# Seven-product v, u and y over super-blocks of 1024 tokens, and LN's small steps for four row tiles at once

## The chip, the cores and the metric

One Trainium2 chip; the kernel runs on one of its cores. The metric is the device time of one execution in microseconds. The core has a matrix engine (TensorE, PE in the profile, with its weight loads as PEld), VectorE (DVE), ScalarE (ACT), GpSimd (POOL) and SyncE (SP), which issues the DMAs here. Each engine works through its own instructions strictly in the order in which they stand and waits at semaphores for the others. TensorE writes to PSUM, eight banks of 128 x 512 float32; the tiles lie in SBUF, 128 partitions wide.

## What is computed

One decoder layer on 2048 tokens of width 1024, all in float32. The mixer is a gated MLP:

```python
h = x * (1.0 + sc1) + sh1                       # sc1, sh1, g1, ... = silu(c) @ mod_w + mod_b
z = gelu(h @ w_in + b_in); u, v = split(z)      # h @ w_in: 2048x1024 by 1024x2048
v = layer_norm(v)                               # over 1024 columns
sv = causal(w_s) @ v, per chunk of 128 tokens and group of 128 columns, + b_s
y = (u * sv) @ w_out                            # 2048x1024 by 1024x1024
x = layer_norm(ALPHA * x + (1.0 + g1) * y)      # "LN1"
h = x * (1.0 + sc2) + sh2
x = layer_norm(ALPHA * x + (1.0 + g2) * ((silu(g) * u2) @ ffn_w_out))   # g, u2 = split(h @ ffn_w_in)
```

## The kernel before

Every float32 operand of a product is split in two parts (`parts`, L90 to L95): ScalarE casts the tile to the matmul's rounded type and VectorE takes the rest, `src - cast`. A product is then three matmuls (hi x hi, hi x lo, lo x hi: `HL`). One matmul is 128 x 128 weights by 128 x 512 columns.

The mixer runs over four blocks of 512 tokens (`NB`, `TB`). In each block `v_part` makes v with `token_major` (8 steps of 24 matmuls into all eight banks, L190 to L206), `us_part` makes u with `feature_major` (8 tiles of 24 matmuls, L208) and, between them, the spatial product `s_tile` and `yT = parts(sv * u)`; `y_part` makes y with `token_major` again. That is 192 matmuls each for v, u and y in a block. The weights wv, wu and wo are loaded and split anew in each block (`load_w`, L97).

LN1 of a block (`norm` in `y_part`, L352 to L367) is done row tile by row tile, 128 tokens each, while TensorE is in the next block's v product: VectorE scales by g1, adds x and takes statistics; `norm_of` (L154) makes the factor with eight small steps on 128 x 1 values, the power on GpSimd; ScalarE normalises; GpSimd multiplies by ln1g and adds ln1b (L364, L366). `h2_part` (L371) transposes the normalised rows on TensorE for the FFN, in the middle of the next block's u (step `h` in the list of L330); the last block's rows are read back from memory in the FFN (`tail`). While the first three blocks run, 48 columns of the modulation are made on VectorE from 512 KB loads each (`mod_col`, L119).

The FFN is already in the seven-product form (Strassen's scheme in Winograd's variant): `h2_part` and `weight` make the sums of quarters on GpSimd (`sub`, L84). It starts with `f_0g_X`, after y's last matmul.

A scheduler orders each engine's instructions when the program is built, from the order of the calls, the tiles' free buffers and its own estimate of times; on the chip the order is fixed. Tiles come from pools with a fixed number of buffers per tag: a new tile waits until the oldest of its tag is released. `late` has 12 buffers of 128 x 1024.

Of the kernel before, what the change touches and what calls it, by code (L numbers as in the profile page):

```python
# [8 lines left out]
F32 = mybir.dt.float32  # L9
# [4 lines left out]
P = 128  # L14
D = 1024
# [21 lines left out]
def gmlp_swiglu_layer(  # L37
# [21 lines left out]
    for side, pad in (("left", 448), ("right", 480)):  # L59
        pads = ctx.enter_context(tc.tile_pool(name=f"pad_{side}", bufs=1, side=side))  # L60
        nc.vector.memset(pads.tile([P, pad // 4], F32, name=f"pad_{side}"), 0.0)
# [34 lines left out]

    def load_w(src, name, tag="raw"):  # L97
        r = new(tag, f"{name}_raw")
        nc.sync.dma_start(out=r, in_=src)
        return [parts(r[:, h * 512 : (h + 1) * 512], f"{name}_{h}", "w") for h in range(2)]  # L100
# [73 lines left out]

    def stats_tile(name, groups=2):
        return small.tile([P, groups, 6], F32, tag=f"st{groups}", name=f"{name}_st", bufs=20 if groups == 2 else 1)
# [13 lines left out]
    def token_major(operands, nk, name, between=()):  # L190

        ps = [[bank(f"{name}_ps{t}{h}") for h in range(2)] for t in range(NT)]
        for k, (a, w) in enumerate(operands):
            for t in range(NT):
                for part, wpart in HL:
                    for h in range(2):
                        nc.tensor.matmul(  # L197
                            ps[t][h],
                            lhsT=a[:, part, t * P : (t + 1) * P],
                            rhs=w[h][:, wpart, :],  # L200
                            start=(k == 0 and part == 0 and wpart == 0),
                            stop=(k == nk - 1 and part == 1),
                        )
            for f in between[k :: nk]:
                f()
        return ps  # L206

    def feature_major(w, rhs, name):  # L208

        ps = bank(name)  # L210
        n = 0
        for d in range(ND):
            for wpart, part in HL:
                nc.tensor.matmul(  # L214
                    ps,
                    lhsT=w[d // 4][:, wpart, (d % 4) * P : (d % 4 + 1) * P],
                    rhs=rhs[d][:, part, :],
                    start=(n == 0),
                    stop=(n == 3 * ND - 1),
                )  # L220
                n += 1
        return ps
# [6 lines left out]
    def start():  # L229
        cact = new("cact", "cact")  # L230
# [7 lines left out]
    def setup_spatial():  # L238

        wm = new("bcv", "wm")  # L240
# [7 lines left out]
        lb = new("raw", "lnb_bc")  # L248
        nc.sync.dma_start(out=lb, in_=lnb.partition_broadcast(P))
        bsr = new("raw", "bs_row")  # L250
        nc.sync.dma_start(out=bsr[0:1, :], in_=bs)
        tb = new("bcv", "tb")
# [10 lines left out]
    def v_operands(b, hT):  # L263
        def operands(d):
            if b == 0:
                sh1[d] = mod_col(0, d, 0.0, "first")
                sc1[d] = mod_col(1, d, 1.0, "first")
            r = new("xh" if b else "first", f"xT{b}_{d}", HALF)
            nc.sync.dma_start(out=r, in_=xT[d, :, b * TB : (b + 1) * TB])
            nc.vector.tensor_scalar(r, r, sc1[d], sh1[d], ALU.mult, ALU.add)  # L270
            hT.append(parts(r, f"hT{b}_{d}", "hT"))
            return hT[d], load_w(wv[d * P : (d + 1) * P, :], f"wv{b}_{d}", "raw" if b else "first")

        return ahead([lambda d=d: operands(d) for d in range(ND)])

    def v_part(b, operands, between):
        ps = token_major(operands, ND, f"v{b}", between)
        if b == 0:
            env["first"].close()
            env["mix"] = phase("left", yT=(8, UNIT), raw=(3, ROW), bcv=(3, ROW), vrow=(4, ROW))  # L280
            env["bv"] = bcast(bv, "bv_bc", "bcv")
# [493 lines left out]
```

## Time and profile before

| what | value |
|---|---|
| median of three runs | 1934.01 us (1925.23 to 1934.22) |
| the profiled execution | 1927.45 us |
| its span, from first to last instruction | 1925.7 us |
| TensorE busy | 1850.6 us, 96% of the span |
| VectorE busy | 1271.0 us, 66% |
| ScalarE, GpSimd busy | 760.3 us, 725.6 us |
| DMA | 312.8 MB, 162 GB/s on average |
| mean granted TensorE clock | 0.983 of full speed |

The mixer takes the first 602 us, the FFN's first product (into `aop`) runs to some 1440 us, the second one and the last LN to the end. Busy times are means over stages with different limits; an engine's idle time matters only where the engine that sets the end waits for it.

### The profile page before, as it was taken

Reading aid. Unit: us, or ns where it says so; the run is one execution under the profiler, and the core shown is the slowest. Engines: PE = TensorE matmul, PEld = TensorE weight load, DVE = VectorE, ACT = ScalarE, POOL = GpSimd, SP = SyncE. Lnnn points to the kernel's source line nnn. Section 1 sums busy time; section 2 is a strip of 40 time slices with the busy share of each in tenths; the row PEclk is TensorE's granted clock in tenths of the full one; section 3 lists DMA queues with packets and bytes.
Section 4 is the critical chain, followed back from the end, with each engine's and each line's share of the span. In section 5 each row is a group of like instructions: output and inputs, shape, how many; then the busy total and the mean of one; then the engine's idle time right before and its main releaser. Section 6 shows DMA issues by size and latency. Waiting matters only on the chain.

```text
span 1925.7 us, 23473 instructions
## 1 busy us (share of the span) xinstructions
PE 1850.6 (96%) x8297; PEld 1532.6 (80%) x8297; DVE 1271.0 (66%) x1857; ACT 760.3 (39%) x1251; POOL 725.6 (38%) x465
## 2 busy tenths in 40 slices
PE   7999999999999999999999999999999999999766
PEld 6887788878888788888887888888888888887655
DVE  8587867686758956555668565556554433576998
ACT  3542543633545434333345333333343444332331
POOL 0000500550402666645644554456432200244844
PEclk9999999999999999999999999999999999999978
DMA  9359446464455444542336323323347644555542
GB/s 354 127 188 326 163 153 227 154 229 158 147 181 186 144 157 153 175 147 94 104 123 202 113 104 115 104 88 110 110 150 253 210 137 142 169 174 171 187 158 109
DMA packets 135065, 312.77 MB, mean 162 GB/s; under 512 B 16642, under 2 KB 21026, under 8 KB 134947
## 3 DMA queue, kind: packets, MB, share of 16 engines
q1 hardware_dynamic: 134882, 311.24, 47.8%
q8 instruction: 65, 1.06, 0.2%
q14 instruction: 54, 0.43, 0.1%
q0 software_dynamic: 64, 0.03, 0.0%
HBM read 239.37 MB, written 71.84 MB: 162 GB/s over the span
## 4 chain that ended last, share of the span: by engine, by line
PE 78%; DVE 13%; DMA 5%; issue 2%; POOL 1%; ACT 1%; SPq 0%; DVEq 0%; POOLq 0%; ACTq 0%
PE o L582 17%; PE u_ps L214 7%; PE y_ps L197 6%; PE v_ps L197 5%; DVE modw L123 2%; PE f_5u_X L433 1%; PE f_4u_X L433 1%; PE f_3u_X L433 1%; PE f_2u_X L433 1%; PE f_9u_X L433 1%; PE f_9g_X L433 1%; PE f_8u_X L433 1%; PE f_8g_X L433 1%; PE f_7u_X L433 1%; PE f_7g_X L433 1%
## 5 line engine op out<-in xcount | busy, mean ns | idle before, releaser
L582 PE MATMUL o<-wd_w,alw 128*128 128x512 f32 (+1 forms) x1881 | 427.9, 390 | 34.9 <-DVE o L82 29.5
L582 PEld LDWEIGHTS o<-wd_w,alw 128*128 128x128 f32 x1881 | 353.8, 191 | 108.9 <-ACT alw L93 23.9
L197 PE MATMUL v_ps<-wv,hT 128*128 128x512 f32 x768 | 179.5, 396 | 16.0 <-ACT wv L93 11.9
L94 DVE TENSOR_TENSOR alw<-al,alw 128x512 fp32r<-128x512 f32 x154 | 126.6, 855 | 94.1 <-ACT alw L93 92.3
L197 PEld LDWEIGHTS v_ps<-wv,hT 128*128 128x128 f32 x768 | 146.5, 191 | 48.1 <-ACT wv L93 12.1
L214 PE MATMUL u_ps<-hT,wu 128*128 128x512 f32 x768 | 181.9, 396 | 0.7 <-ACT h L388 0.5
L197 PE MATMUL y_ps<-wo,yT 128*128 128x512 f32 x768 | 177.0, 392 | 3.9 <-DVE sv L320 3.9
L197 PEld LDWEIGHTS y_ps<-wo,yT 128*128 128x128 f32 x768 | 144.9, 189 | 34.3 <-issue 4.3
L214 PEld LDWEIGHTS u_ps<-hT,wu 128*128 128x128 f32 x768 | 144.9, 191 | 31.3 <-issue 0.8
L161 POOL TENSOR_TENSOR ln_rs<-ln_ve,mhalf 128x1 f32<-128x1 f32 x32 | 27.3, 860 | 357.5 <-DVE ln_ve L159 346.2
L93 ACT CAST alw<-al 128x512 fp32r<-128x512 f32 x154 | 88.8, 619 | 146.3 <-PE o L582 117.7
L85 POOL TENSOR_TENSOR chain<-wd,chain 128x512 f32<-128x512 f32 x22 | 34.6, 1576 | 157.4 <-DMA wd<-in_wd 154.6
L94 DVE TENSOR_TENSOR wu<-wu_raw,wu 128x512 fp32r<-128x512 f32 x64 | 59.5, 946 | 50.5 <-ACT wu L93 50.1
L93 ACT CAST wv<-wv_raw 128x512 fp32r<-128x512 f32 x64 | 37.6, 620 | 98.0 <-PE v_ps L197 43.0
L123 DVE SCALAR_TENSOR_TENSOR modw<-modw,cact 128x1024 f32<-128x1024 f32 x48 | 58.3, 1218 | 19.0 <-DMA modw<-in_modwT 19.0
L94 DVE TENSOR_TENSOR wv<-wv_raw,wv 128x512 fp32r<-128x512 f32 x64 | 47.5, 761 | 21.8 <-ACT wv L93 21.7
L94 DVE TENSOR_TENSOR wo<-wo_raw,wo 128x512 fp32r<-128x512 f32 x64 | 46.8, 742 | 19.8 <-ACT wo L93 19.8
L94 DVE TENSOR_TENSOR wd_w<-wd,wd_w 128x512 fp32r<-128x512 f32 x44 | 37.1, 842 | 34.5 <-ACT wd_w L93 34.5
L93 ACT CAST wo<-wo_raw 128x512 fp32r<-128x512 f32 x64 | 38.5, 616 | 43.2 <-PE y_ps L197 42.1
L93 ACT CAST wu<-wu_raw 128x512 fp32r<-128x512 f32 x64 | 38.1, 616 | 35.2 <-PE v_ps L197 18.9
L93 ACT CAST wd_w<-wd 128x512 fp32r<-128x512 f32 x44 | 27.3, 621 | 47.7 <-PE o L582 35.7
L364 POOL TENSOR_TENSOR r<-r,ln1g_bc 128x1024 f32<-128x1024 f32 x16 | 42.4, 2665 | 10.0 <-ACT r L173 10.0
(606 smaller groups left out, 3870.7 us busy)
## 6 DMA issues: line engine op xcount, KB each, us to landing
al<-aop SPq DMA_DIRECT2D x154, 256.0 KB, 3.3
wd<-in_wd SPq DMA_DIRECT2D x99, 256.0 KB, 3.3
modw<-in_modwT SPq DMA_DIRECT2D x48, 512.0 KB, 8.1
aop<-aop_s SPq DMA_DIRECT2D x88, 256.0 KB, 2.0
wv_raw<-in_wv SPq DMA_DIRECT2D x32, 512.0 KB, 5.0
wu_raw<-in_wu SPq DMA_DIRECT2D x32, 512.0 KB, 4.1
wo_raw<-in_wo SPq DMA_DIRECT2D x32, 512.0 KB, 3.6
hop<-h SPq DMA_DIRECT2D x40, 256.0 KB, 3.1
```

Source lines behind the costliest of these rows:

```text
L85: nc.gpsimd.tensor_tensor(out=o, in0=a, in1=b, op=ALU.subtract)
L93: nc.scalar.copy(out=o[:, 0, :], in_=src)
L94: nc.vector.tensor_tensor(out=o[:, 1, :], in0=src, in1=o[:, 0, :].bitcast(F32), op=ALU.subtract)
L123: nc.vector.scalar_tensor_tensor(out=w, in0=w, scalar=1.0, in1=env["cact"], op0=ALU.mult, op1=ALU.mult, accum_out=modc[:, j : j + 1],)
L161: nc.gpsimd.tensor_tensor(out=rs, in0=ve, in1=mhalf, op=ALU.pow)
L197: nc.tensor.matmul(ps[t][h], lhsT=a[:, part, t * P : (t + 1) * P], rhs=w[h][:, wpart, :], start=(k == 0 and part == 0 and wpart == 0), sto ...
L214: nc.tensor.matmul(ps, lhsT=w[d // 4][:, wpart, (d % 4) * P : (d % 4 + 1) * P], rhs=rhs[d][:, part, :], start=(n == 0), stop=(n == 3 * ND ...
L364: nc.gpsimd.tensor_tensor(out=r, in0=r, in1=env["ln1g"], op=ALU.mult)
L433: nc.tensor.matmul(ps, lhsT=w[:, wpart, k * P : (k + 1) * P], rhs=a[k][:, part, :], start=(first and k == 0 and wpart == 0 and part == 0), ...
L582: nc.tensor.matmul(ps[:, cs], lhsT=a[:, part, p * P : (p + 1) * P], rhs=w[:, wpart, cs], start=(first and part == 0 and wpart == 0), stop= ...
```

## The change

The mixer runs over two super-blocks of 1024 tokens (`mixer(sb, before)`), and v, u and y are each made by seven products on quarters: 512 tokens x 512 inputs (four tiles of 128 inputs, `k`) by 512 inputs x 512 outputs, 48 matmuls each, 12 per `k`. `left_ops` makes the sums of the left quarters (of h, shared by v and u, and of u * sv), `right_ops` those of the weights, both on GpSimd; `combine` adds up the results, on VectorE from PSUM and, after products 6 and 7, on GpSimd from SBUF. The order is `SEVEN`, v and u in turn up to product 3, then v 7, v 4, u 7, u 4. The spatial tiles of a super-block's first half stand in u 7, those of the second in u 4 and y 1. LN1 of the first half is called after y's product 3 and its `h2_part` in y's product 4; LN1 of the second half in the next super-block's v 1 and u 1, its `h2_part` in v 2. `norm_rows` makes the factors of four row tiles in one set of small steps on 128 x 4 values, for the LN of v and LN1; it begins when all four have their statistics. The modulation's columns are all made in the first super-block. The FFN is as before.

```diff
+    def norm_rows(tiles, sts, name):
+        m = len(tiles)
+        mv = sm("mvs", [m, 2])
+        for t in range(m):
+            nc.vector.bn_aggr(out=mv[:, t, :], in_=sts[t])
+        ve, rs, nw, nm = (sm(tag, [m]) for tag in ("ves", "rss", "nws", "nms"))
+        nc.vector.tensor_scalar(ve, mv[:, :, 1], EPS, None, ALU.add)
+        nc.gpsimd.tensor_tensor(out=rs, in0=ve, in1=mhalf.broadcast_to([P, m]), op=ALU.pow)
...
+        for t in range(m):
+            nc.scalar.activation(tiles[t], tiles[t], AF.Identity, bias=nm[:, t : t + 1], scale=rs[:, t : t + 1])
...
+    SEVEN = (1, 2, 5, 6, 3, 7, 4)
+    def left_ops(raw, name):
...
+            if pr == 5:
+                a21, a22 = quarter(1, 0, k), quarter(1, 1, k)
+                s1[k] = new("half", f"{name}_s1{k}")
+                nc.gpsimd.tensor_tensor(out=s1[k], in0=a21, in1=a22, op=ALU.add)
+                sub(a21, a11, a21)
+                sub(a11, s1[k], a11)
+                sub(a12, a12, a11)
+            src = {1: (0, 0), 6: (0, 0), 2: (0, 1), 3: (0, 1), 7: (1, 0), 4: (1, 1)}.get(pr)
+            return parts(a[(*src, k)] if src else s1[k], f"{name}_S{pr}{k}", "S")
+    def right_ops(w, name):
...
+            if pr == 5:
+                t = chain[k] = load(0, 1, k, "chain")
+                sub(t, t, load(0, 0, k))
+            elif pr in (6, 4):
+                t = chain[k]
+                sub(t, load(1, 1 if pr == 6 else 0, k), t)
+            elif pr == 7:
+                t = load(1, 1, k)
+                sub(t, t, load(0, 1, k))
+            else:
+                t = load(1 if pr > 1 else 0, 1 if pr == 3 else 0, k)
+            return parts(t, f"{name}_T{pr}{k}", "w")
+    def combine(pr, ps, cell, bias=None):
+        for j in range(4):
...
+            else:
+                add(cell(1, 0, j), ps[j], cell(1, 0, j))
+            if pr in (6, 7):
+                o = cell(*((0, 1) if pr == 6 else (1, 1)), j)
+                nc.gpsimd.tensor_tensor(out=o, in0=cell(1, 0, j), in1=cell(1, 1, j), op=ALU.add)
...
+        steps = [(m, pr) for pr in SEVEN[:5] for m in "vu"] + [("v", 7), ("v", 4), ("u", 7), ("u", 4)]
...
+        during["u", 7] = s_tiles(0, *range(8))
+        during["u", 4] = s_tiles(1, *range(4, 8))
+        made = ahead([lambda m=m, pr=pr, k=k: operands(m, pr, k) for m, pr in steps for k in range(NK)], 3)
...
+        for pr in SEVEN:
+            ps = [bank(f"y{sb}_{pr}_{j}") for j in range(4)]
+            if pr == 4:
+                during[4] = h2_parts(blocks[0], [rows[0, t] for t in range(NT)])
...
+            combine(pr, ps, cell_y)
+            if pr == 3:
+                for f in norms(blocks[0], [rows[0, t] for t in range(NT)]):
+                    f()
...
+        def final():
+            norm_rows(rows, sts, f"ln1_{b}")
+            for t, r in enumerate(rows):
+                nc.gpsimd.tensor_tensor(out=r, in0=r, in1=env["ln1g"], op=ALU.mult)
+                e = nc.vector if b == NB - 1 else nc.gpsimd
+                e.tensor_tensor(out=r, in0=r, in1=env["ln1b"], op=ALU.add)
...
+    mix = phase(
+        "left", S=(10, UNIT), w=(5, UNIT), braw=(4, HALF), chain=(8, HALF), bc=(4, ROW), h2=(2, ROW), sv=(2, HALF),
+    )
+    early = phase("right", half=(26, HALF))
...
+    rows = mixer(0, before)
+    steps = norms(1, rows)
+    before = {("v", 1): steps[:NT], ("u", 1): steps[NT:], ("v", 2): h2_parts(1, rows)}
+    rows = mixer(1, before)
```

How the instructions stand now is told at three places. In the names, `v0_5_2` is v of super-block 0, product 5, fourth-part 2; `h0_S51` a split left operand of product 5, k 1; `wv0_T51` a split right one; `r0_3` row tile 3 of block 0 for LN1.

GpSimd at the start of the first super-block. Before, the first row is the causal mask of w_s (`wm`), and after it come the powers of LN:

```order
L243 AFFINE_SELECT wm_746<-wm_746 128x1024
L161 TENSOR_TENSOR lnv0_0_rs_824<-lnv0_0_ve_822,mhalf_83 128x1
L161 TENSOR_TENSOR lnv0_1_rs_883<-lnv0_1_ve_881,mhalf_83 128x1
L161 TENSOR_TENSOR lnv0_2_rs_942<-lnv0_2_ve_940,mhalf_83 128x1
L161 TENSOR_TENSOR lnv0_3_rs_962<-lnv0_3_ve_960,mhalf_83 128x1
```

Now, in the same place (`xT0_0` and its like are the scaled h quarters, `wv0_b010` weight quarters):

```order
L313 AFFINE_SELECT wm_509<-wm_509 128x1024
L226 TENSOR_TENSOR h0_s10_767<-xT1_0_761,xT1_4_764 128x512
L85 TENSOR_TENSOR xT1_0_761<-xT0_0_342,xT1_0_761 128x512
L85 TENSOR_TENSOR wv0_b010_775<-wv0_b010_775,wv0_b000_777 128x512
L85 TENSOR_TENSOR xT0_0_342<-h0_s10_767,xT0_0_342 128x512
L85 TENSOR_TENSOR wv0_b011_817<-wv0_b011_817,wv0_b001_819 128x512
L85 TENSOR_TENSOR xT0_4_545<-xT0_4_545,xT0_0_342 128x512
L226 TENSOR_TENSOR h0_s11_809<-xT1_1_803,xT1_5_806 128x512
```

Between the mask and the first power of LN there now stand 50 sums of 128 x 512.

TensorE at the transposes of block 0's rows. Before, they stand among block 1's u tiles:

```order
L214 MATMUL u1_3_ps_2183<-hT1_7_1887,wu1_3_1_2113 128x512 x3
L387 MATMUL h2T0_0_ps_2211<-ident_76,r0_0_1562 128x128
L387 MATMUL h2T0_0_ps_2211<-ident_76,r0_1_1563 128x128
L387 MATMUL h2T0_0_ps_2211<-ident_76,r0_2_1564 128x128
L387 MATMUL h2T0_0_ps_2211<-ident_76,r0_3_1565 128x128
```

Now they stand behind y's last product of the super-block, in the order of the rows and over all eight banks, and the next super-block's v comes after them:

```order
L267 MATMUL y0_4_2_2782<-wo0_T43_2790,y0_S43_2784 128x512 x3
L267 MATMUL y0_4_3_2783<-wo0_T43_2790,y0_S43_2784 128x512 x3
L497 MATMUL h2T0_0_ps_2806<-ident_76,r0_0_2325 128x128
L497 MATMUL h2T0_4_ps_2812<-ident_76,r0_0_2325 128x128
L497 MATMUL h2T0_1_ps_2833<-ident_76,r0_0_2325 128x128
```

The end of the same run of 32 transposes, whose last eight read r0_3:

```order
L497 MATMUL h2T0_6_ps_2866<-ident_76,r0_3_2331 128x128
L497 MATMUL h2T0_3_ps_2887<-ident_76,r0_3_2331 128x128
L497 MATMUL h2T0_7_ps_2893<-ident_76,r0_3_2331 128x128
L267 MATMUL v1_1_0_2942<-wv1_T10_2917,h1_S10_2912 128x512 x3
L267 MATMUL v1_1_0_2942<-wv1_T11_2928,h1_S11_2923 128x512 x3
```

The transposes of block 2 stand in the same way between y's last product of the second super-block and the FFN's first matmul, where before the FFN followed y at once.

GpSimd at LN1 of block 0. Before, each row tile has its own power and its multiplication and addition follow:

```order
L161 TENSOR_TENSOR ln1_0_3_rs_1826<-ln1_0_3_ve_1824,mhalf_83 128x1
L364 TENSOR_TENSOR r0_0_1562<-r0_0_1562,ln1g_bc_1234 128x1024
L364 TENSOR_TENSOR r0_1_1563<-r0_1_1563,ln1g_bc_1234 128x1024
L364 TENSOR_TENSOR r0_2_1564<-r0_2_1564,ln1g_bc_1234 128x1024
L366 TENSOR_TENSOR r0_0_1562<-r0_0_1562,ln1b_bc_1236 128x1024
```

Now:

```order
L182 TENSOR_TENSOR ln1_0_rss_2656<-ln1_0_ves_2655,mhalf_83 128x4
L468 TENSOR_TENSOR r0_0_2325<-r0_0_2325,ln1g_bc_1513 128x1024
L468 TENSOR_TENSOR r0_1_2327<-r0_1_2327,ln1g_bc_1513 128x1024
L468 TENSOR_TENSOR r0_2_2329<-r0_2_2329,ln1g_bc_1513 128x1024
L470 TENSOR_TENSOR r0_0_2325<-r0_0_2325,ln1b_bc_1515 128x1024
L468 TENSOR_TENSOR r0_3_2331<-r0_3_2331,ln1g_bc_1513 128x1024
L470 TENSOR_TENSOR r0_1_2327<-r0_1_2327,ln1b_bc_1515 128x1024
L470 TENSOR_TENSOR r0_2_2329<-r0_2_2329,ln1b_bc_1515 128x1024
L182 TENSOR_TENSOR ln1_1_rss_3079<-ln1_1_ves_3078,mhalf_83 128x4
L470 TENSOR_TENSOR r0_3_2331<-r0_3_2331,ln1b_bc_1515 128x1024
```

Block 1's power (`ln1_1_rss`) has moved ahead of block 0's last addition. In block 2 both powers stand first, and r2_3's addition is the twelfth wide operation behind them.

## Rows read from the trace of the kernel before

**Rows 1.** Stage table: length, busy time and count of each engine, clock, DMA share, GB/s.

```profile
core 0: us, PE busy (x) PEld busy (x) DVE busy (x) ACT busy (x) POOL busy (x), PEclk, DMA share, GB/s
0.00:602.00 602.00, 578.41 (x2689) 481.55 (x2690) 434.64 (x804) 260.73 (x407) 126.34 (x86) 0.99 0.57 198
700.00:1400.00 700.00, 697.50 (x3089) 577.16 (x3088) 416.02 (x463) 275.30 (x472) 364.85 (x232) 1.00 0.37 125
```

**Rows 2.** Timeline of TensorE: start, length, engine, line, output and inputs, count.

```profile
11.88 46.08 PE L197 MATMUL v_ps<-wv,hT 128*128 128x512 f32 x192 [11.88 <-ACT wv L93]
...
63.97 29.11 PE L214 MATMUL u_ps<-hT,wu 128*128 128x512 f32 x120
...
504.12 22.02 PE L214 MATMUL u_ps<-hT,wu 128*128 128x512 f32 x96
525.98 3.65 PE L387 MATMUL h2T_ps<-ident,r 128*128 128x128 f32 x32
...
558.35 43.78 PE L197 MATMUL y_ps<-wo,yT 128*128 128x512 f32 x192
601.97 2.88 PE L433 MATMUL f_0g_X<-h2A,f_0g_w 128*128 128x512 f32 x12
```

**Rows 3.** Timeline of VectorE in the first block, GpSimd idle.

```profile
6.64 1.23 DVE L123 SCALAR_TENSOR_TENSOR modw<-modw,cact 128x1024 f32<-128x1024 f32 x1 [5.32 <-DMA modw<-in_modwT]
...
14.30 1.22 DVE L123 SCALAR_TENSOR_TENSOR modw<-modw,cact 128x1024 f32<-128x1024 f32 x1
...
15.44 0.33 DVE L127 TENSOR_SCALAR modc<-modc,modbc 128x1 f32<-128x1 f32 x2
15.81 0.55 DVE L270 TENSOR_SCALAR xT<-xT,modc 128x512 f32<-128x512 f32 x1
16.27 1.29 DVE L94 TENSOR_TENSOR wv<-wv_raw,wv 128x512 fp32r<-128x512 f32 x2
17.48 1.22 DVE L123 SCALAR_TENSOR_TENSOR modw<-modw,cact 128x1024 f32<-128x1024 f32 x1
```

**Rows 4.** Timelines of GpSimd and of VectorE in the same 3 us of the FFN.

```profile
764.17 1.28 POOL L411 TENSOR_TENSOR aop_s<-aop_s,f_3g_c 128x512 f32<-128x512 f32 x1
765.42 1.74 POOL L85 TENSOR_TENSOR f_4g_b<-f_4g_b,f_4g_b 128x512 f32<-128x512 f32 x1
...
764.30 1.71 DVE L94 TENSOR_TENSOR f_4u_w<-f_4u_b,f_4u_w 128x512 fp32r<-128x512 f32 x1
765.93 1.77 DVE L503 TENSOR_TENSOR f_3g_u<-f_3g_u,f_3u_u 128x512 f32<-128x512 f32 x1
```

**Rows 5.** Groups by line: count, busy us, mean ns of one, idle before.

```profile
L364 POOL TENSOR_TENSOR r<-r,ln1g_bc 128x1024 f32<-128x1024 f32 x12 | 31.4, 2632 | 8.5 <-ACT r L173 8.5
L173 ACT ACTIVATE r<-r,ln_nm,ln_rs 128x1024 f32<-128x1024 f32 x12 | 14.2, 1235 | 3.9 <-DVE ln_nm L172 3.8
L286 DVE TENSOR_TENSOR v<-v_ps,bv_bc 128x512 f32<-128x512 f32 x32 | 20.0, 676 | 7.8 <-PE v_ps L197 7.8
L166 DVE TENSOR_TENSOR lnv_rs<-lnv_rs,lnv_nw 128x1 f32<-128x1 f32 x16 | 2.3, 153 | 0.0
```

**Rows 6.** The same stretch, line L94 on VectorE alone: its busy time and count.

```profile
700.00:1400.00 700.00, 286.38 (x283) 1.00 0.37 125
```

**Rows 7.** The tail, 1800 to 1926 us: stage table, then VectorE's groups by line.

```profile
1800.00:1926.00 126.00, 84.99 (x382) 70.24 (x380) 117.51 (x171) 31.78 (x46) 69.86 (x41) 0.83 0.40 139
...
L94 DVE TENSOR_TENSOR alw<-al,alw 128x512 fp32r<-128x512 f32 x26 | 27.2, 1064 | 1.0 <-ACT alw L93 1.0
L539 DVE TENSOR_TENSOR o<-o,ln2b_bc 128x1024 f32<-128x1024 f32 x12 | 21.7, 1809 | 2.4 <-POOL o L538 2.4
...
L166 DVE TENSOR_TENSOR ln_rs<-ln_rs,ln_nw 128x1 f32<-128x1 f32 x12 | 9.8, 822 | 0.6 <-DVE ln_nw L165 0.5
...
L164 DVE SCALAR_TENSOR_TENSOR ln_nw<-ln_rs,ln_ve 128x1 f32<-128x1 f32 x11 | 8.7, 788 | 0.2 <-POOL ln_rs L161 0.2
```

**Rows 8.** DMA issues: queue, count, KB each, median us from issue to landing.

```profile
x<-in_x SPq DMA_DIRECT2D x16, 512.0 KB, 6.5
```

**Rows 9.** Stage table around the tail's gap on TensorE, columns as in rows 1.

```profile
1840.00:1850.00 10.00, 5.44 (x11) 3.38 (x12) 10.00 (x12) 2.79 (x5) 7.54 (x6) 0.52 0.66 233
```

## What the change does to the time: the prediction

> **What bounds the kernel now.** I read the stage table first. Up to 602 us, where the mixer ends, TensorE is busy for 578 us, and in the FFN's first product (700 to 1400) for 697.5 of 700 us: TensorE's instruction stream sets the time. VectorE works 435 us and GpSimd only 126 us in the mixer; ScalarE has 261 us [rows 1]. TensorE's own timeline gives the pieces, each row a run of like matmuls. 192 matmuls of 512 columns take 43.62 us from start to start (558.35 to 601.97), so 0.2272 us each. A block's spatial products and h2 transposes are the rest of 504.12 to 558.35: 54.23 - 43.62 = 10.6 us, of which the transposes take 3.6 and s_tile's matmuls 7.0; the first block also has 6.1 us of small matmuls for tb before its u products [rows 2]. The FFN's first matmul stands at 601.97 us. Nothing behind that point is changed, so I predict the shift of that matmul and add it to the profiled execution's 1927.45 us. (The three runs' median is 1934.01, 0.34% above it. About 0.5% is what a measurement of this kernel can tell from no change.)
>
> **What goes away.** Each 1024-token block has 7 quarter products of 48 matmuls in place of 8 for each of v, u and y: 2016 matmuls where there were 2304. 288 x 0.2272 = 65.4 us less for TensorE. The rest of its work stays, so a TensorE that never waited would start the FFN at 11.9 + 2016 x 0.2272 + 4 x 7.0 + 6.1 + 3 x 3.6 = 515 us.
>
> **What comes in.** VectorE's steps, from start to start: 1.14 us for a 1024-wide op on two SBUF tiles (a column of mod), 0.37 / 2 = 0.185 us for its small add, 0.46 us for xT's scale, 1.21 / 2 = 0.605 us for one splitting [rows 3]. An add from PSUM has the same recorded length as a splitting (676 ns against 680 to 690) [rows 5], so 0.605 as well; bn_stats is put there too. In the new order of VectorE, everything up to the last weight part of y's product 4 in the first super-block is: 144 splittings, 61 adds from PSUM, 18 bn_stats, 16 scalings of s and 16 u*sv = 255 x 0.605 = 154.3; 48 mods and 5 other wide ops x 1.14 = 60.4; 48 x 0.185 = 8.9; 23 x 0.46 = 10.6; some 25 tiny ones at 0.1 (an estimate) = 2.5. Sum 236.7 us, from the first mod at 6.6 us [rows 3]: 243.3 if VectorE never waits. TensorE alone would come to the end of that product at 11.9 + 229.0 + 14.0 + 6.1 = 261 us, plus the 2.5 us by which the first 192 matmuls exceed 43.6 [rows 2]. So only some 20 us of slack are left for all waits.
>
> The waits come from GpSimd. It now makes the sums of the seven products: 101 adds of 128x512 up to the same point, where the kernel before has next to none in its first block. The trace shows that such an add and a VectorE op with two SBUF inputs do not overlap: GpSimd takes 1.28 us when it comes first, then 1.74 us with a splitting between, and the VectorE ops beside it take 1.71 and 1.77 us where 0.68 is their length alone [rows 4]. What this costs VectorE per GpSimd op is the disputed price. In the FFN's calm stage 283 splittings take 286.4 us, 0.32 us above 0.69 each, 91 us in all over 232 GpSimd ops: 0.39 us per op [rows 1, 6]. In the tail, where VectorE is never idle as it would be here, the excess of four groups (26 x 0.37, 12 x 0.59, 12 x 0.67, 11 x 0.64 us over lengths alone of 0.69, 1.22 and 0.15 [rows 3, 5]) is 31.9 us over 69.9 us of GpSimd: 0.46 us per us, 0.58 for an op of 1.28 us, and more with the smaller groups that I left out [rows 7]. The bounds are 0.39 and the whole 1.28. I take 0.65, nearest to the tail. Then 101 x 0.65 = 66 us come on top, 243.3 + 66 = 309, and with the last 12 matmuls (2.7 us) y's product 4 ends at E = 312 us.
>
> The Trainium skill (SBUF — State Buffer, section Who interferes with whom) says that a VectorE instruction with two SBUF inputs and a GpSimd instruction that reads SBUF exclude each other, the second one blocking until the first is done, and that one with a single SBUF input is free. By it the sum would have a floor: (144 + 16) x 0.605 + 53 x 1.14 + 101 x 1.28 = 286.5 us of exclusive use from 6.6 us on, E at 296 or later, if all work from PSUM hid behind GpSimd. By the rows it is 312.
>
> **First hole.** In TensorE's new order the 32 transposes of block 0's h2 stand between y's product 4 and v of the second super-block; the last eight read r0_3. On GpSimd the last op of r0_3 stands behind the pow of block 1's LN, and that needs all four rows of block 1, which are complete only at E. From E (its first bank is done 2 us earlier) VectorE has 18 ops x 0.605, 9 wide x 1.14 and 14 tiny ones, 22.6 us, until block 1's variance; block 0's coefficients are ready after 15 of them. ScalarE then needs 1.2 us and GpSimd eight ops of 2.63 us and a pow of about 1 us [rows 5]: -2 + 15 + 1.2 + 22 + 1 of transposes = 37 us. The x rows have one free buffer, so each load starts only when the row before is added, and four loads of 4 to 6.5 us [rows 8] stand in that stretch; this adds 0 to 8 us. I take 40. After a gap of 23 us the trace shows TensorE at a granted clock of 0.52, 11 matmuls taking 5.4 us in place of 2.5 [rows 9]: 3 us more. v of the second super-block starts at 312 + 43 = 355.
>
> **Second super-block.** TensorE: 1008 x 0.2272 + 14.0 + 3.6 = 246.6 us. VectorE, without mods: 241 x 0.605 + 5 x 1.14 + 9 x 0.46 + 2 = 157.6, with 120 GpSimd adds at 0.65 = 78, behind the first v product (8.6) and with 2.7 at the end: 246.9. They tie; the end is at 602.
>
> **Second hole.** The same 32 transposes, of block 2, now stand ahead of the FFN's first matmul. On GpSimd both LN pows come first and then twelve ops on 1024 columns, with r2_3's last. VectorE: 22 x 0.605 + 10 x 1.14 + 1.4 - 2 = 24; ScalarE 1.2; pows 2; 12 x 2.63 = 31.6; transposes 1: 60 us, and 3 for the clock. Before, this work lay under the FFN's matmuls.
>
> The FFN starts at 602 + 63 = 665 in place of 602: 1927.45 + 63 = **1990 us**. Costed at nothing: the extra loads (36 quarters of 256 KB for a weight per super-block, where there were 32), under a DMA share of 0.57 in the mixer [rows 1], though the first 50 us are nearly full; ScalarE's 24 more casts; the small LN steps, which were beside TensorE's work in any case. If loads come late in the first 100 us, each microsecond goes on E.
>
> **Rivals.** (1) VectorE keeps pace: the price falls to 0.2 us or less (0.2 is 20 us over 101 adds). Then only the holes count: 264 + 43 + 247 + 63 = 617, 15 us later, 1942 us. For it: the calm stage's 0.39 is not far. Against: VectorE would need no other wait. (2) Faster: TensorE's count decides. That needs the price of (1), and holes that sum to less than 85 us in place of 106. With holes halved (53 us) the FFN starts at 564 and the time is 1890. For it: TensorE's 96% in the mixer [rows 1]. Against: the order in which the engines stand, which is fixed. (3) Full exclusion: 1.0 us per add in both super-blocks. E = 243.3 + 101 + 2.7 = 347, the second 157.6 + 120 + 11.3 = 289, and 347 + 43 + 289 + 63 = 742: 140 us later, 2067. For it: single GpSimd ops make VectorE wait for all of 1.1 us [rows 4]. (4) The price stays at 0.39: E = 285, FFN at 638, 1963; this is inside my case.
>
> **How the numbers follow.** My case (price 0.39 to 0.9, both holes): 0.67. Rival 1: 0.12. Rival 2: 0.08. Rival 3 or worse: 0.13. The time is my case's. The range takes in rival 1 and most of rival 3: 1940 to 2065. Faster by over 0.5% is rival 2 and a little of 1: 0.09. Within 0.5% (up to 1943.7) is half of rival 1: 0.07. Slower: 0.84.
>
> **What would show it.** Right: from about 60 us on, TensorE's idle time is released by VectorE's and GpSimd's parts of products 5, 6, 7 and 4; VectorE is near 100% busy in the first super-block; two gaps of about 40 and 60 us ahead of h2T's transposes, released by GpSimd's last add of LN1; a low granted clock behind each; matmul groups of the mixer near 458 us; the FFN unchanged once it runs. Wrong: y's product 4 ending near 264 us, or gaps under 25 us, or stalls released by DMA.

## The result, and the profile after

The changed kernel takes 2116.68 us (median of 4, 2108.85 to 2118.94) where the kernel before, beside it, takes 1930.97: a ratio of 1.0958, 95% interval 1.0916 to 1.1. Slower, as forecast, but by 9.6% where 1990 us was 3.2%; the time lies above the range of 1940 to 2065.

The stage table of the profiled execution after (columns as in [rows 1]), cut where the stages change: the first 49 us, the first super-block with these, the first gap, the second super-block, the second gap, the FFN's first product.

```profile
0.00:49.00 49.00, 33.34 (x128) 25.75 (x128) 32.72 (x62) 13.36 (x21) 4.82 (x11) 0.96 0.98 374
0.00:356.00 356.00, 280.48 (x1168) 220.67 (x1168) 314.85 (x456) 127.12 (x204) 171.32 (x115) 0.93 0.59 191
356.00:410.00 54.00, 8.29 (x34) 6.65 (x34) 37.03 (x55) 11.00 (x11) 31.34 (x15) 0.53 0.33 116
410.00:712.00 302.00, 263.00 (x1168) 213.97 (x1167) 239.51 (x284) 124.59 (x201) 200.60 (x129) 0.93 0.44 142
712.00:787.00 75.00, 7.87 (x32) 6.27 (x32) 52.27 (x67) 16.93 (x21) 46.71 (x23) 0.51 0.36 126
850.00:1400.00 550.00, 546.74 (x2422) 452.66 (x2420) 330.13 (x367) 219.82 (x376) 289.01 (x184) 1.00 0.39 132
```

From 850 us on, TensorE is as full as it was [rows 1]. The loss lies ahead of the FFN. TensorE's timeline shows the two gaps (in brackets the idle time before a row, and what released it):

```profile
392.23 1.97 PE L497 MATMUL h2T_ps<-ident,r 128*128 128x128 f32 x8 [36.19 <-POOL r L470]
397.81 1.97 PE L497 MATMUL h2T_ps<-ident,r 128*128 128x128 f32 x8 [3.62 <-POOL r L470]
400.12 1.97 PE L497 MATMUL h2T_ps<-ident,r 128*128 128x128 f32 x8 [0.34 <-POOL r L470]
403.41 1.97 PE L497 MATMUL h2T_ps<-ident,r 128*128 128x128 f32 x8 [1.32 <-POOL r L470]
409.62 13.13 PE L267 MATMUL v<-wv_T,h_S 128*128 128x512 f32 x48 [4.24 <-ACT h L498]
...
759.54 1.97 PE L497 MATMUL h2T_ps<-ident,r 128*128 128x128 f32 x8 [47.60 <-POOL r L470]
...
787.32 5.49 PE L543 MATMUL f_0g_X<-h2A,f_0g_w 128*128 128x512 f32 x12 [4.51 <-ACT h L498]
```

y's product 4 ends at 356.0, v of the second super-block starts at 409.6, that super-block ends at 711.9, and the FFN starts at 787.3, against 601.97 before [rows 2]:

| step | predicted | measured | difference |
|---|---|---|---|
| end of the first super-block | 312 | 356.0 | +44 |
| first gap (predicted: 40, and 3 for the clock behind it) | 43 | 53.6 | +11 |
| second super-block | 247 | 302.3 | +55 |
| second gap (predicted: 60, and 3 for the clock) | 63 | 75.4 | +12 |
| the FFN from there on | as before | 6 more | +6 |

That is 128 us, all of the way from 1990 to this execution's 2118.9. (What the clock took behind each gap, 2 to 3 us, is not in the measured gaps but in the row below each: the second super-block and the FFN.) Both gaps are where they were foretold, released by GpSimd's last addition of LN1 (L470). The two super-blocks are the larger error, and the experiments are mostly about them.

### The profile page after: what moved, and what is told of

Its sections match the earlier page's. It is cut to its first block, busy times and chain, and to the rows that moved or that the text cites. A ratio compares the mean times of both kernels' runs of the same rounds, so it can differ in the third digit from the quotient of the medians.

```text
span 2117.1 us, 23383 instructions
## 1 busy us (share of the span) xinstructions
PE 1838.0 (87%) x8009; PEld 1502.8 (71%) x8009; DVE 1450.6 (69%) x1869; ACT 781.0 (37%) x1283; POOL 1032.0 (49%) x650
## 4 chain that ended last, share of the span: by engine, by line
PE 55%; DVE 4%; DMA 2%; issue 1%; ACT 0%; POOL 0%; DVEq 0%; SPq 0%; POOLq 0%; ACTq 0%
PE o L692 16%; PE f_0g_X L543 1%; DVE alw L94 1%; PE f_5u_X L543 1%; PE f_4u_X L543 1%; PE f_3u_X L543 1%; PE f_2u_X L543 1%; PE f_9g_X L543 1%; PE f_8u_X L543 1%; PE f_8g_X L543 1%; PE f_7u_X L543 1%; PE f_7g_X L543 1%; PE f_6u_X L543 1%; PE f_6g_X L543 1%; PE f_5g_X L543 1%; PE f_4g_X L543 1%
## 5 line engine op out<-in xcount | busy, mean ns | idle before, releaser
L267 PE MATMUL v<-wv_T,h_S 128*128 128x512 f32 x672 | 175.5, 417 | 49.7 <-ACT h_S L93 15.9
L267 PEld LDWEIGHTS v<-wv_T,h_S 128*128 128x128 f32 x672 | 134.0, 202 | 86.8 <-ACT h_S L93 17.1
L94 DVE TENSOR_TENSOR alw<-al,alw 128x512 fp32r<-128x512 f32 x154 | 126.2, 852 | 94.4 <-ACT alw L93 92.6
L267 PE MATMUL y<-wo_T,y_S 128*128 128x512 f32 x672 | 164.8, 403 | 21.6 <-DVE wo_T L94 19.9
L269 PE MATMUL u<-h_S,wu_T 128*128 128x512 f32 x672 | 169.6, 408 | 12.7 <-DVE wu_T L94 10.1
L267 PEld LDWEIGHTS y<-wo_T,y_S 128*128 128x128 f32 x672 | 128.8, 194 | 53.3 <-DVE wo_T L94 24.1
L269 PEld LDWEIGHTS u<-h_S,wu_T 128*128 128x128 f32 x672 | 130.9, 198 | 45.5 <-DVE wu_T L94 12.9
L85 POOL TENSOR_TENSOR wo_b<-wo_b,wo_b 128x512 f32<-128x512 f32 x32 | 52.0, 1632 | 71.5 <-DMA wo_b<-in_wo 58.9
L94 DVE TENSOR_TENSOR wu_T<-wu_b,wu_T 128x512 fp32r<-128x512 f32 x56 | 63.2, 1141 | 11.9 <-ACT wu_T L93 11.9
L94 DVE TENSOR_TENSOR wv_T<-wv_b,wv_T 128x512 fp32r<-128x512 f32 x56 | 58.0, 1041 | 16.7 <-ACT wv_T L93 16.5
L94 DVE TENSOR_TENSOR wo_T<-wo_b,wo_T 128x512 fp32r<-128x512 f32 x56 | 59.8, 1075 | 8.9 <-ACT wo_T L93 8.6
L94 DVE TENSOR_TENSOR wd_w<-wd,wd_w 128x512 fp32r<-128x512 f32 x44 | 36.5, 828 | 35.8 <-ACT wd_w L93 35.8
```

Of the source, the lines that this page charges most:

```text
L85: nc.gpsimd.tensor_tensor(out=o, in0=a, in1=b, op=ALU.subtract)
L94: nc.vector.tensor_tensor(out=o[:, 1, :], in0=src, in1=o[:, 0, :].bitcast(F32), op=ALU.subtract)
L267: nc.tensor.matmul(ps[j], lhsT=a[:, p, js], rhs=w[:, q, :], start=first, stop=last)
L269: nc.tensor.matmul(ps[j], lhsT=w[:, p, js], rhs=a[:, q, :], start=first, stop=last)
```

## Experiments

The four runs of the changed kernel lie within 10 us (0.5%), so a single run says little of a few us. "End" is the end of y's product 4 in the first super-block, 356 us in the changed kernel. All edits are made in the changed kernel.

### The sums, and who pays for them

**e1**, the seven products without GpSimd's sums:

```diff
-                nc.gpsimd.tensor_tensor(out=s1[k], in0=a21, in1=a22, op=ALU.add)
-                sub(a21, a11, a21)
-                sub(a11, s1[k], a11)
-                sub(a12, a12, a11)
+                s1[k] = a21
...
-                sub(t, t, load(0, 0, k))
+                load(0, 0, k)
...
-            if pr in (6, 7):
-                o = cell(*((0, 1) if pr == 6 else (1, 1)), j)
-                nc.gpsimd.tensor_tensor(out=o, in0=cell(1, 0, j), in1=cell(1, 1, j), op=ALU.add)
```

> The changed kernel with all of GpSimd's sums for the seven products left out, those of the left and right operands and those that combine the results (so what it computes is not the layer); loads, splittings, VectorE's adds from PSUM and all matmuls stay. Theory A: VectorE sets the pace of the first super-block and each GpSimd sum costs it about 0.70 us there (71 us over some 101). Then y's product 4 ends near 285 us instead of 356, the second super-block takes about 270 instead of 302, and the run comes to about 2015. Theory B: the stalls come from the chain of load, cast and splitting with few buffers and not from GpSimd. Then y's product 4 still ends past 335 us and the run is over 2085. Both gaps ahead of h2's transposes stay (50 and 75 us) under either.

Measured: 2007.16 us, end at 299, second super-block 264, gaps of 46 and 71. Theory A, with 57 of its 71 us at the end. Its stage table over the two super-blocks:

```profile
0.00:300.00 300.00, 266.08 (x1168) 215.55 (x1168) 247.71 (x465) 126.92 (x205) 7.57 (x13) 0.96 0.67 229
346.00:609.00 263.00, 251.03 (x1167) 209.71 (x1167) 179.50 (x288) 125.16 (x202) 43.62 (x28) 0.97 0.50 165
```

Between the stretches to 356 and to 300 us, VectorE's busy time falls from 314.9 to 247.7 us: 67.1 us over 102 sums, 0.66 us each. In e1 nine VectorE operations more (6.3 us) stand in its stretch; without them a sum costs 0.72. VectorE's groups by form in the changed kernel, 49 to 356 us, and then in e1, 49 to 300, show which operations pay:

```profile
L94 DVE TENSOR_TENSOR wo_T<-wo_b,wo_T 128x512 fp32r<-128x512 f32 x28 | 29.2, 1048 | 5.3 <-ACT wo_T L93 5.2
L343 DVE TENSOR_SCALAR xT<-xT,modc 128x512 f32<-128x512 f32 x18 | 18.9, 1076 | 0.0
L82 DVE TENSOR_TENSOR v<-v,v 128x512 f32<-128x512 f32 x20 | 12.5, 680 | 0.0
```

```profile
L94 DVE TENSOR_TENSOR wo_T<-wo_b,wo_T 128x512 fp32r<-128x512 f32 x28 | 19.2, 686 | 10.0 <-ACT wo_T L93 10.0
L335 DVE TENSOR_SCALAR xT<-xT,modc 128x512 f32<-128x512 f32 x18 | 9.1, 540 | 1.6 <-DMA xT<-in_xT 1.6
L82 DVE TENSOR_TENSOR v<-v,v 128x512 f32<-128x512 f32 x20 | 13.0, 683 | 2.7 <-PE v L262 2.7
```

The splitting (two SBUF inputs) takes 1048 ns beside the sums and 686 without, and the scaling of xT twice its length; the add from PSUM (v) costs nothing more. The Trainium skill (SBUF — State Buffer, section Who interferes with whom) counts VectorE's operations with two SBUF inputs among those that exclude GpSimd, and tensor_scalar too where it runs in a two-port mode; an operation with at most one SBUF input outside these modes is free. The trace agrees in the rows of the splitting and of the add; in the row of xT it agrees if that scaling ran in such a mode, which no row shows. My prediction had said that one SBUF input is free, without that condition, and xT's scaling, which has one, was not: 1076 ns beside the sums, 540 without.

**e2**, the same sums on VectorE (`nc.gpsimd.tensor_tensor` and `sub` become `nc.vector.tensor_tensor` at these places):

> The same sums made by VectorE instead of GpSimd. Theory A (VectorE's time is the bound, in sum): 101 x 0.605 = 61 us of own work replace some 71 us of price, so y's product 4 ends near 345 us, the second super-block is 0 to 15 us shorter, and the run comes to about 2095. Theory B (what hurts is the time that a sum takes on GpSimd on the way to TensorE, 1.5 to 1.9 us each, one behind the other): y's product 4 ends before 320 us and the run is at 2050 or less. If VectorE was already full and the price was little, it gets slower: 2150.

Measured: 2083.37 us, end at 342, second super-block 295, gaps of 49 and 70. Theory A by the end, a little better by the total. Made by VectorE itself, the sums put the end 43 us behind that of e1; made by GpSimd, 57. The 14 us between the two are hardly more than the end moves in e9 and e10 below, where no work is changed.

**e3**, VectorE without most modulation columns:

```diff
+        if k > 1:
+            return modc[:, j : j + 1]
         nc.vector.scalar_tensor_tensor(
```

> The changed kernel without VectorE's two operations for 32 of the 48 modulation columns (g1, sh2, sc2, g2, which are set to 1, so the output is not the layer's); their loads stay. VectorE loses 32 x 1.64 = 52 us in the first super-block. Theory A (VectorE sets the pace there): y's product 4 ends near 305 us instead of 356, nothing behind it changes (302 us for the second super-block), the run comes to about 2065. Theory B (TensorE waits there for loads and for the chain of small steps, not for VectorE's sum): it ends past 340 us, the run is over 2100.

Measured: 2079.58 us, end at 318, second super-block 304. Of some 48 us of busy time taken off VectorE, 38 come out at the end: theory A, with a fifth lost to new waits.

**e9 and e10**, look-ahead of two and of four steps (`ahead(..., 3)` becomes 2, 4):

> The changed kernel with operands made two steps ahead of the matmuls instead of three; the same instructions. My prediction took the fuller engine (VectorE) to set the end of the first super-block by its sum. If it does, the depth matters little: y's product 4 ends at 356 plus or minus 5, the run is at 2117 plus or minus 10. If the waits come from the chain load, GpSimd, ScalarE, VectorE within the few steps that are made ahead, it ends 15 to 40 us later and the run is at 2150 or more.

> The same with four steps ahead. Sum theory: no change, 2117 plus or minus 10. Chain theory: y's product 4 ends 10 to 20 us earlier, the second super-block is some 10 us shorter, the run is at 2090 or less, unless the few buffers (5 split weights, 4 raw quarters) hold it back, in which case both depths above 2 look alike.

Measured: 2110.55 us with two steps (end 343, second super-block 310) and 2102.82 with four (344 and 301). The chain theory fails for two steps: the end comes earlier and not 15 to 40 us later, and the total is within the scatter of the changed kernel's runs. With four steps the end comes 12 us earlier, as that theory has it, but the total stays 13 us above its 2090. That both ends come 12 to 13 us earlier is neither theory's; an order that is moved a little moves the end that much, and I can't say more of it. VectorE's row up to the end, in e3, e9 and (below) e12:

```profile
0.00:318.00 318.00, 270.02 (x1168) 218.17 (x1168) 266.95 (x361) 126.78 (x204) 168.91 (x115) 0.94 0.65 214
```

```profile
0.00:343.00 343.00, 279.77 (x1168) 221.82 (x1168) 306.67 (x455) 127.01 (x203) 181.00 (x116) 0.92 0.60 198
```

```profile
0.00:346.00 346.00, 279.21 (x1166) 221.45 (x1167) 306.49 (x566) 128.77 (x205) 6.82 (x13) 0.90 0.60 199
```

Counted from its first wide operation at 6.6 us, VectorE is idle for 35 us in the changed kernel, 46 in e1, 44 in e3, 30 in e9 and 33 in e12. In all eleven kernels here that have all seven products it is 20 to 46 us, with 247 to 322 us of work; the least idle time stands beside the most work (e7) and the most beside the least (e1).

### The gaps

**e4**, the transposes of blocks 0 and 2 moved:

```diff
-                during[4] = h2_parts(blocks[0], [rows[0, t] for t in range(NT)])
...
+    before.setdefault(('u', 1), []).extend(h2_parts(0, rows0))
+    before.setdefault(('v', 2), []).extend(h2_parts(1, rows))
...
+    between = {((2, 3, 4, 5)[i], 1): lambda i=i: tail(NB - 2, i) for i in range(NK)}
+    between.update({((6, 7, 8, 9)[i], 1): lambda i=i: tail(NB - 1, i) for i in range(NK)})
```

> The transposes of block 0's h2 moved behind u's product 1 of the second super-block, those of block 2 into the FFN beside block 3's; all else as changed. Theory A (the two gaps are TensorE waiting in order for LN1 of blocks 0 and 2, with nothing else late): the second gap goes (75 us, less some 10 of new stalls as the FFN starts), the first shrinks by the 22 us of v's and u's product 1 that now run under it; the run comes to about 2030. Theory B (VectorE and GpSimd are behind as a whole, so that the wait comes back as stalls in the products): the run is over 2085.

Measured: 2086.95 us, just past theory B's bound. The first gap and the second super-block, 355.9 us together, became 349.4: TensorE ran v's and u's first product at once, and then stood 60 us in all for block 0's and block 1's transposes. The FFN starts 84 us earlier, but 37 of these are left at its fifth pass. The stage from the FFN's start on, and its longest waits:

```profile
704.00:785.00 81.00, 42.31 (x120) 26.83 (x118) 73.37 (x84) 29.20 (x43) 50.52 (x24) 0.72 0.48 162
```

```profile
PE f_0g_X L541 <- DVE h2S L94: 12.0, 3, 6.6
PE f_0g_Z L541 <- DVE h2S L94: 10.9, 2, 8.5
```

VectorE is 91% busy there with LN1 of blocks 2 and 3 and splits the FFN's own operands late. So a gap was not only a wait in the wrong place; some of that work was late itself.

**e11**, LN1's gain and bias of blocks 0 and 2 on VectorE:

```diff
-                nc.gpsimd.tensor_tensor(out=r, in0=r, in1=env["ln1g"], op=ALU.mult)
-                e = nc.vector if b == NB - 1 else nc.gpsimd
+                f = nc.gpsimd if b % 2 else nc.vector
+                f.tensor_tensor(out=r, in0=r, in1=env["ln1g"], op=ALU.mult)
+                e = nc.gpsimd if b == 1 else nc.vector
```

> The changed kernel with LN1's gain and bias of blocks 0 and 2 on VectorE instead of GpSimd (a 1024-wide operation takes 1.22 us there against 2.63). Theory (each gap is a chain of statistics, power, scaling and then eight wide operations in a row): each gap shrinks by some 10 us, 53.6 to 43 and 75.4 to 65, the run comes to about 2097. Rival (VectorE, still busy with residuals and splittings, and the loads of x set the gap's end): no change, or slower.

Measured: 2098.45 us, gaps of 40.1 and 60.9 us. As expected: the wide operations are links of the chain that ends a gap. The gaps give 28 us; the second super-block takes 12 of them back (313.8 us).

**e7**, LN's small steps for each row tile (`norm_rows(rows, sts, ...)` becomes `normalise(r, sts[t], ...)` in a loop, at both places):

> The changed kernel with LN's small steps made for each row tile again, for v and for LN1. Theory A (GpSimd's eight wide operations of a block wait in the gap for the fourth row's statistics, so a power for each row lets the first of them start some 15 us earlier): each gap shrinks by 10 to 15 us, the run comes to about 2095. Rival (VectorE's many small steps are what the form for four rows saves, and the gap's end is set by the last row in any case): 2117, or slower by up to 10 us.

Measured: 2116.84 us (ratio to before 1.0975, 1.0925 to 1.1025; the changed kernel's is 1.0958). The rival: this half of the change does nothing that can be measured in the total. The first gap is 53.6 us here too, the second 79.2.

**e13**, block 1's h2 sums on VectorE (`e = nc.vector if b == 1 else nc.gpsimd` for the four sums of `h2_part`):

> The changed kernel with the 16 sums of block 1's h2 operands on VectorE instead of GpSimd. In the second super-block TensorE waits 19 us around the transposes of block 1, each part of which needs the two h2 buffers that GpSimd's sums of the part before hold. Theory D (those sums stand behind the seven products' sums on GpSimd, and VectorE has time there, 79% busy): the waits fall to 5 us or less, the second super-block from 302 to some 288, the run to about 2103. Rival (loads and stores of the h2 buffers hold them, or VectorE is behind as well): 302 plus or minus 4, run 2117 plus or minus 6.

Measured: 2103.77 us, as by theory D, but the second super-block only came to 296, and the FFN started only 7 us earlier; the rest came behind that, which the theory has no reason for. TensorE's waits ahead of these transposes in the changed kernel (410 to 712 us), and here (395 to 700) with one that is new:

```profile
PE h2T_ps L497 <- ACT h L498: 12.7, 1, 12.7
PE h2T_ps L497 <- DVE v L82: 6.3, 1, 6.3
```

```profile
PE h2T_ps L497 <- DVE v L82: 10.1, 1, 10.1
...
PE v L267 <- DVE v L82: 4.9, 1, 4.9
```

Half of theory D: the wait for ScalarE's copy, which the theory lays to GpSimd's sums, goes; those behind VectorE grow.

### The parts of the change

**e5**, eight products in the same frame; **e6**, y alone with seven; **e8**, v and u alone with seven. The core of the eight:

```diff
+            for z in range(2):
+                for k in range(NK):
+                    a, w = next(made)
...
+            groups = [(m, x, y) for x in range(2) for m in "vu" for y in range(2)]
```

> The changed kernel with eight quarter products in place of seven for v, u and y, in the same frame: super-blocks of 1024 tokens, quarters of a weight, four banks a group, LN for four rows at once. No sums on GpSimd, no adds on VectorE to combine; 288 matmuls (65.4 us) more. Theory A (the loss is the seven form's sums and the order that it forces on the rows of block 0 and 2): each super-block takes TensorE's 276 us and some 10 of stalls, and since block 0's rows are complete two groups (43 us) ahead of the end, the gaps shrink to some 15 and 25 us. FFN's start near 635 us, the run at about 1960. Theory C (the frame itself loses most: quarters loaded and split in small steps, LN1 and h2 standing between the super-blocks): the run is at 2030 or more.

> As e5, but y's product takes seven products again, v and u eight. TensorE's count falls by 96 matmuls, 21.8 us against e5. Theory A: y takes about 99 us a super-block as in the changed kernel, where eight products take some 91, so 2 x 8 us are lost in y, and the two gaps come back at 50 and 75 us, since the rows of block 0 and 2 are complete only two products ahead of the end; with about 1960 for e5 this gives some 2060. Rival: y's stage has VectorE time to spare and the gaps are the frame's, so the 21.8 us come out: 20 us faster than e5.

> The counterpart of e6: v and u take seven products, y eight, all in the frame of e5. If the costs of the parts simply add, then against e5 (FFN's start at 646 us) v and u cost what they cost between e6 and the changed kernel, 787 - 736 = 51 us, and the gaps stay small as in e5: FFN's start near 697, the run at 2030. If v's and u's sums only hurt together with y's (GpSimd and VectorE behind), the 192 matmuls less (43.6 us) come out at least in part: 1960 or less.

| kernel | time, us | ratio to before | end | first gap | second super-block | second gap | FFN's start |
|---|---|---|---|---|---|---|---|
| e5, eight everywhere | 1983.01 | 1.0281 (1.0243 to 1.032) | 320.1 | 5.8 | 294.9 | 25.5 | 646.4 |
| e6, y seven | 2069.09 | 1.0728 (1.0691 to 1.0764) | 316.3 | 54.3 | 288.1 | 77.7 | 736.3 |
| e8, v and u seven | 2041.14 | 1.0587 (1.0556 to 1.0618) | 352.2 | 6.3 | 317.1 | 15.1 | 690.6 |
| changed, all seven | 2116.68 | 1.0958 (1.0916 to 1.1) | 356.0 | 53.6 | 302.3 | 75.4 | 787.3 |

e5 lies between its two theories, nearer A; e6 and e8 came within 11 us of theirs. In FFN starts, the frame costs 44 us, y's seven products 90 more, v's and u's 44 more, and 7 come from the two together. The total times say 53, 86 and 58, and the two together cost 10 less than their sum: e8's FFN starts early and then waits 22 us in its first passes, where the changed kernel's waits 5. Its longest wait, and that of e5's second gap, which is the FFN's own weight and not LN1:

```profile
PE f_0g_Z L628 <- ACT h2S L93: 15.2, 1, 15.2
```

```profile
PE f_0g_X L628 <- ACT f_0g_w L93: 18.1, 1, 18.1
```

y's seven products take a little off the super-blocks (4 and 7 us, where the count says 10.9 each) and bring the gaps back. (Where there are eight products, y's results in e5 and e8 and u's in e5 and e6 also leave PSUM by ScalarE, not VectorE.) In e5 the first gap is all but gone. In TensorE's timeline of e5 the transposes stand among y's last matmuls, and the next v follows:

```profile
313.80 0.60 PE L582 MATMUL h2T_ps<-ident,r 128*128 128x128 f32 x4
...
325.94 45.40 PE L416 MATMUL v<-wv_w,hT 128*128 128x512 f32 x192 [2.74 <-ACT h L583]
```

With eight products a quarter of y is finished group by group, so block 0's rows are complete two groups (43 us) ahead of the end, and LN1's power runs at 294.18 us, 26 us ahead of it. With seven they need five of the seven products, and only two (22 us) are left. In the changed kernel that power runs 22 us behind the end:

```profile
377.72 1.02 POOL L182 TENSOR_TENSOR ln_rss<-ln_ves,mhalf 128x4 f32<-128x4 f32 x1 [18.06 <-DVE ln_ves L181]
```

v's and u's seven products, in turn, make no gap but lengthen the super-blocks, by 32 and 22 us, in spite of 21.8 us less of matmuls in each.

**e12**, all repairs in one kernel (the edits of e2, e4, e10 and e11):

> All repairs that the earlier runs point to, in one kernel: the seven products' sums on VectorE (-34 us alone), LN1's gain and bias of blocks 0 and 2 on VectorE (-18), the h2 transposes of these blocks later (-30), operands four steps ahead (-14). If the losses were separate, the gains add: 2117 - 96 = 2021 or a little less. If they are one loss, VectorE and TensorE in turn waiting for each other, less than two thirds come: 2050 or more. At or below 1931, the kernel before, it would show that the seven products can pay here; I don't expect it.

Measured: 2049.10 us, ratio to before 1.0612 (1.055 to 1.0673): 68 of the 96 us, just above the two thirds that I had set apart as the limit. The losses are partly the same loss, and the sum of all repairs does not make up for the change. No kernel here is faster than before; the fastest, e5, has no seven products in the mixer at all.

## Why the prediction was right in sign and wrong in size

**The gain.** 65.4 us of matmuls less is right as a count: a super-block's stage shows 1168 matmuls, of which 1008 are products. None of it reached the end, since TensorE waits or runs at a low clock for more than that.

**The price of a sum.** 0.65 us was taken between bounds of 0.39 and 1.28; e1 gives 0.66 to 0.72 in the first super-block, and (239.5 - 179.5) / 104 = 0.58 in the second, where it leaves out 104 of the 120 sums (the 16 of h2 stay). This step held; since 0.65 was taken from another stage, the tail, that it fits so closely is partly luck.

**VectorE's sum as the end.** This is the step that failed: "243.3 if VectorE never waits", and then 312 with the price and nothing else. The busy time was nearly right: 236.7 + 66 = 303 predicted, 315 measured, 12 of the 44 us. But 35 us of idle time come on top, where the sum had none but the first 6.6 us, and the runs above have 20 to 46 us in each. e1 shows it without any price: its end is at 299, where 243.3 + 2.7 = 246 was the sum and 264 TensorE's. Some of the idle time I had named and costed at nothing: "If loads come late in the first 100 us, each microsecond goes on E". In the first 49 us VectorE is busy for only 32.7 of 42.4 us from its first operation on, at a DMA share of 0.98: 10 of the 35 us. The rest is waits for other engines, in pieces. VectorE's longest waits up to 352 us (in total, times, longest; 5.3 of the first row's 9.0 us stand ahead of 6.6 us):

```profile
DVE modw L118 <- DMA modw<-in_modwT: 9.0, 4, 5.3
DVE lnv_nws L184 <- POOL lnv_rss L182: 5.6, 1, 5.6
DVE wo_T L94 <- ACT wo_T L93: 5.2, 3, 2.4
DVE h_S L94 <- ACT h_S L93: 4.6, 2, 3.9
```

What sets these waits stays open. One rival that no run tests is the chain of loads with few buffers behind ScalarE's casts; in e1, where VectorE waits 14 us for the casts of wu, ScalarE waits for their loads (0 to 300 us):

```profile
DVE wu_T L94 <- ACT wu_T L93: 14.2, 5, 7.3
ACT wu_T L93 <- DMA wu_b<-in_wu: 32.3, 11, 8.7
```

Rival 3 came nearer, for the first super-block (347) and for the total (2067), by a wrong reason: the price was not 1.0.

**The tie in the second super-block.** TensorE 246.6 and VectorE 246.9 were to end together at 247. VectorE's busy time is 239.5, so its sum was again right, and it set nothing: the stage took 302. TensorE's 1168 matmuls, the predicted 246.6 us, show 263.0 of busy time; the other 39 us it waits, and VectorE 62. So the tie's sum, which let each engine's waits lie under the other's work, is what failed here; that two engines which hand each other tiles in order add up their waits is my reading, and no run tests it alone. What the waits are is known in part: 19 us ahead of block 1's transposes (e13 takes 9 of them away by moving GpSimd's sums), 8 for wo_T, the rest in pieces.

**The clock.** I priced it at 3 us behind each gap. There it is right: the 48 matmuls after the first gap, whose row has a granted clock of 0.53, take 13.13 us where 10.9 is their rate. But short stalls went with a low clock too. After a stand of 3 us in the second super-block 14 matmuls took 6.30 us where 3.2 is their rate, in a stretch at the lower of the two levels, 1.2 GHz (granted clock 0.51); the stretch before it, with TensorE busy for 24.9 of 27 us, had 1.00 (the matmuls' row of the timeline, then the stage rows of the two stretches):

```profile
499.87 6.30 PE L269 MATMUL u<-h_S,wu_T 128*128 128x512 f32 x14 [2.96 <-DVE wu_T L94]
...
472.00:499.00 27.00, 24.91 (x110) 20.28 (x108) 17.95 (x17) 10.60 (x17) 25.97 (x18) 1.00 0.64 186
499.00:506.00 7.00, 6.13 (x14) 4.80 (x15) 7.00 (x8) 3.48 (x7) 6.92 (x6) 0.51 0.31 109
```

In the first super-block 1168 matmuls are busy for 280.5 us instead of 249.1 (229.0 + 14.0 + 6.1), in the second 16 us too long, at a mean granted clock of 0.93 in both; without sums (e1, clock 0.96 and 0.97) the excess is 17 and 4. I had no term for that. In the second super-block it is part of the end; in the first, as far as VectorE paces, it hides under VectorE (argued, not shown).

**The gaps.** 53.6 and 75.4 us against 43 and 63: right in place, releaser and chain. In the first, block 0's coefficients are ready 24 us after the end and not 13 (their power runs at 22), since VectorE first makes operands of the next super-block; GpSimd's eight wide operations take 22 us as foretold; and 4.2 us that I had left out pass until ScalarE has emptied the banks that the next v needs (last row of the first gap). In the second the powers come at 746.85, 35 us behind the end where I had 24, behind splittings for the FFN.

**The small LN steps**, costed at nothing, cost nothing that the total shows (e7).

**The rivals.** That TensorE's count decides, and that VectorE keeps pace, fell with the first two rows of the table. None of the rivals held both super-blocks' waits.

## What to carry to other kernels

A form with fewer matmuls is paid for on the engines that make its operands: sum their busy time, but don't let the fuller engine's sum stand for the end, since in the eleven kernels counted here 20 to 46 us of idle time came on top of 247 to 322 us of work, and a stage whose two engines were to tie took 55 us more than either's sum. Ask of a seven-product form when each row of the result is complete, because what follows it (here LN1 and the transposes) lost its cover: y's seven products alone cost 86 us of the total and brought both gaps back, v's and u's cost 58 and brought none. Before building such a change, the same frame with the old form (e5) and each product alone (e6, e8) tell the frame's cost and that of each product apart in three runs.

## What the runs showed of the hardware

A step of four elements can be as dear as a wide one: one of LN's small VectorE steps took 948 ns on average beside GpSimd's sums, where the same step takes 154 ns in e1, without the sums. In the changed kernel, 49 to 356 us, and in e1, 49 to 300:

```profile
L184 DVE TENSOR_TENSOR lnv_nws<-lnv_rss 128x4 f32<-128x4 f32 x2 | 1.9, 948 | 5.6 <-POOL lnv_rss L182 5.6
```

```profile
L184 DVE TENSOR_TENSOR lnv_nws<-lnv_rss 128x4 f32<-128x4 f32 x2 | 0.3, 154 | 0.0
```

In e7 TensorE was full at a recorded clock of 1.00 in the FFN and yet slower than in the changed kernel: in the same 300 us, first there and then in e7,

```profile
1250.00:1550.00 300.00, 300.00 (x1325) 248.51 (x1324) 170.68 (x190) 111.25 (x189) 152.25 (x96) 1.00 0.31 106
```

```profile
1250.00:1550.00 300.00, 300.00 (x1314) 246.19 (x1313) 169.22 (x188) 108.99 (x186) 149.53 (x94) 1.00 0.30 102
```

A pass of the FFN took 38.4 us in e7 and 38.1 there, with the same instructions. It ate the 5 us by which e7's FFN had started earlier. Why is open.
